# A transformer-style block chain with its residual stream kept token-major instead of feature-major

## The chip, the cores and the metric

One core of a Trainium2 chip. The metric is the device time of one execution in microseconds (us), the median of several runs. TensorE (PE) multiplies matrices, VectorE (DVE) and ScalarE (ACT) do the elementwise work, GpSimd (POOL) clears a few tiles, and SyncE (SP) issues nearly all DMAs.

## The reference, cut to what matters

256 tokens of 1024 features, all float32. Two layers of a first block, then one layer of a second block:

```python
h = x
for layer in range(2):
    xn = rms_norm(h, attn_norm_g[layer])
    ...                                   # SSM, spatial gating, differential attention
    h = h + mixed @ w_out[layer]          # 1024 x 1024
    xn = rms_norm(h, ffn_norm_g[layer])
    h = h + conv_gated_mlp(xn, w_up[layer], conv_w[layer], conv_b[layer], w_down[layer])   # w_down: 2816 x 1024
# second block: h2 = rms_norm(h, g_pre); three attention branches; merged; then
x = h + rms_norm(merged @ w_out_2, g_post)
```

The convolution runs along the tokens. The second block's attention over dilated windows is computed with the tokens in another order (t mod 4, t div 4 mod 4, t div 16).

## The kernel before

The program is traced through a scheduling layer that turns one list of operations into one instruction queue for each engine. Within a queue the order is fixed; between queues semaphores wait. Each operation has a priority, its place in the list; `later(tc, n)` moves it back by n places.

**Products.** Every large product is made exact by splitting both factors into a high and a low float32r part and adding three matmuls: high by high, high by low, low by high. The class `Stream` loads each weight by a 1 MB DMA on SP's queue (`wraw`, three buffers) and splits it in pieces of 128x1024 ahead of use: ACT writes `whi` (line 152), DVE writes `wlo` (line 153); there are five buffers of each, and four pieces are split ahead. Activations X are split in the same way into `xh` and `xl` (`split_scaled`, lines 664 and 665; `split_plain`, lines 668 and 669). All matmuls of a product go through `Bank.mm`, so they stand at line 94, and are told apart by their tiles: `acc` and `ps` are PSUM banks.

**Two layouts.** `mm_xs` makes token-major results: 128 tokens of X are stationary and 256 or 512 weight columns move. `mm_ws` makes feature-major ("d-major") results: a 128x128 piece of the weight is stationary and the 256 tokens of X move. The residual stream `h` is d-major, [128, 8, 256].

**w_out and w_down.** Both are written out inside `layer`, in the d-major manner: eight row blocks of w_out, or 22 of w_down (two for each j of `down`), times eight column blocks of 128, times three matmuls of 256 moving columns. Four banks `acc` collect the result. In layer 0, 16 identity matmuls first put x, turned to d-major, into the banks. In w_out one piece of the weight is used up after another; in w_down the two pieces of a j are held together while the banks are gone through one after the other.

**residual** (line 1198) follows each of these four products: a DVE addition for each bank (line 1206; none in layer 0's w_out, where ACT copies the bank at line 1216), the split into the next X (two for each bank), a Square on ACT (line 1213), a DVE addition of its halves (line 409), and in `Stats.add` two matmuls of one column against `ones` that sum the squares over the features. `Stats.finish` calls `norm_from`: the chain of small DVE operations of `rsqrt` (lines 373 to 383), two matmuls that spread the result over partitions (line 693), an ACT copy `rstdB` (line 696). The next products' results are scaled by `rstdB` or `rstd` when they are read out of PSUM; in the MLP that is the DVE operation of line 1342, which frees one of two `ps` banks.

**Around it.** After w_out comes `up(0)`, two products of 48 matmuls into the two `ps` banks. After layer 0's last `down`, `mem_keys` (96 matmuls) stands ahead of `residual`. After layer 1's last `down` comes the second block, whose `a_half` starts with products into `acc`; `x2_gen` (line 1440) transposes h back to token-major, 16 transposes and four copies, for the last addition. The token order of the second block is made by strided copies in layer 1: of h in `residual` (`permute`) and of the gated product in `up`. At the end, each tile q of 128 tokens is stored by two DMAs (line 1811) whose rows are picked out of the output in the other order.

Of the kernel before, what the change touches and what calls it, by code (L numbers as in the profile page):

```python
# [11 lines left out]
F32 = mybir.dt.float32  # L12
# [8 lines left out]
P = 128  # L21
S = 256
# [75 lines left out]
class Stream:  # L98
    """The weights in the order of their use: loaded, and split into two float32r parts, ahead of it."""
# [67 lines left out]
def tile_model(tc, t, out):  # L167
# [54 lines left out]
    # ------------------------------------------------------------------ weights in order of use  # L222
# [12 lines left out]
    # products of the mixers (lower case) and their generators' steps  # L235
# [58 lines left out]
    # ------------------------------------------------------------------ constants and small inputs  # L294
# [4 lines left out]
    ones = const.tile([P, 2], F32, name="ones")  # L299
    V.memset(ones, 1.0)  # L300
# [9 lines left out]
    def param_rows(*ps, eng=nc.sync):  # L310
        """Parameter rows -> columns of pvt."""
# [95 lines left out]
    # ------------------------------------------------------------------ first block: SSM parameters  # L407
# [12 lines left out]
    def ssm_params():  # L420
# [27 lines left out]
        # half angle -> full angle, then onto the unit circle  # L448
# [14 lines left out]
        # f = (a_bar - 1) / lambda  # L463
# [28 lines left out]
    def ssm_prep(l):  # L492
        """Segments of 4 tokens: A^i B-bar, C A^k, the 4-tap kernels Re(C A^i B-bar), the rotation table
        e^(-4 i theta m), m < 64, and the scan's multipliers."""
# [14 lines left out]
        def cmul(o, x, y, tv):  # L509
            """o = x * y for (re, im) pairs, tv scratch of o's shape."""  # L510
# [12 lines left out]
        # C^T, states on partitions, expanded with zeros and compact  # L523
# [15 lines left out]
        # powers of A, 0 to 4, and their products with f  # L539
# [23 lines left out]
        # C A^k, k from 1 to 4, the imaginary part negated  # L563
# [15 lines left out]
        # A^i B-bar; stacked as (channel, i) rows by states, and times C for the taps  # L579
# [40 lines left out]
        # rotation table  # L620
# [28 lines left out]
    # ------------------------------------------------------------------ token order of block 2  # L649
# [6 lines left out]
    # ------------------------------------------------------------------ normalisation helpers  # L656
# [14 lines left out]
    class Stats:  # L671
        """Sums of squares over d (rows of the d-major tiles) per token."""

        def __init__(self):
            self.b = psx()
            self.n = 0

        def add(self, sq):
            self.n += 1
# [5 lines left out]
        def finish(self):  # L685
# [1157 lines left out]
```

## Time and profile before

| | us |
|---|---|
| median of 3 runs (lowest, highest) | 1073.31 (1072.55, 1074.68) |
| span of the profiled execution, first to last instruction | 1071.4 |
| PE busy, and its weight loads (PEld) | 1028.5 and 956.9 |
| DVE busy, ACT busy | 779.0 and 624.1 |
| chain that ended last, share of PE | 85% |
| HBM read, over the span | 160.15 MB, 150 GB/s |

The profiled execution's time outside its span is not listed; its span is 1.9 us under the median of the runs. PE's busy time counts each matmul from its start to the end of its pipeline, so that neighbours overlap: what a matmul costs in a dense row is the distance between starts, read from a timeline or from a run of matmuls in the chain.

The stages stand in the span like this: layer 0's mixers to about 128 us, its w_out to 147.5, its MLP to 367.4, layer 1's mixers to 471, w_out to 487, MLP to 683.7, the second block to 1055.6, then the last norm and the stores.

### The profile page before, as it was taken

The numbers are of one execution on the slowest core, as the hardware profiler recorded it, in microseconds if no ns is written. First come the engines' busy times: TensorE is split into PE (matmuls) and PEld (weight loads), VectorE is DVE, ScalarE is ACT, GpSimd is POOL, SyncE is SP. The second block draws the span as 40 slices with busy tenths as digits, with TensorE's granted clock in tenths as the row PEclk, the third lists the DMA queues.
The fourth block names the chain that finished last, engine by engine and source line by source line (L and its number), as shares of the span: only waits on it lengthen the run. The fifth ranks groups of instructions, "written<-read, shape, count | busy, mean of one in ns | idle before, by whom it ended". The sixth has DMA issues, their size and how long they took to land.

```text
span 1071.4 us, 19616 instructions
## 1 busy us (share of the span) xinstructions
PE 1028.5 (96%) x7751; PEld 956.9 (89%) x7751; DVE 779.0 (73%) x1577; ACT 624.1 (58%) x1206; POOL 14.3 (1%) x34
## 2 busy tenths in 40 slices
PE   7799999999999999998999999999999999999994
PEld 5678898999999988888999999999787899899993
DVE  6978769877888769658878787876665666546663
ACT  5876567655665667657655555645675555444450
POOL 2000000000000000100000000000000000000000
PEclk9899999999999999999999999999999999999997
DMA  7542253555655445135556555468332546336531
GB/s 200 194 141 91 63 173 118 191 172 185 222 177 193 158 131 191 66 124 170 164 176 207 169 190 193 152 184 275 121 119 80 167 114 195 112 113 192 164 137 39
DMA packets 130484, 166.66 MB, mean 156 GB/s; under 512 B 12034, under 2 KB 103256, under 8 KB 130392
## 3 DMA queue, kind: packets, MB, share of 16 engines
q1 hardware_dynamic: 130360, 165.40, 47.9%
q8 instruction: 61, 1.00, 0.4%
q14 instruction: 31, 0.25, 0.1%
q10 hardware_dynamic: 32, 0.01, 0.0%
HBM read 160.15 MB, written 1.05 MB: 150 GB/s over the span
## 4 chain that ended last, share of the span: by engine, by line
PE 85%; DVE 7%; ACT 4%; issue 1%; DMA 1%; SPq 0%; POOL 0%; ACTq 0%; POOLq 0%; DVEq 0%
PE acc L94 50%; PE ps L94 26%; PE px L94 2%; DVE sgen L409 2%; DVE wlo L153 1%; PE pt L1506 1%; ACT sgen L600 1%; ACT whi L152 1%; ACT gen L1005 1%; PE px L905 1%; PE acc L1561 1%; DMA wraw<-in_w_in_dram 1%; PE acc L1652 1%; PE pt L1124 0%; DVE gen L1331 0%
## 5 line engine op out<-in xcount | busy, mean ns | idle before, releaser
L152 ACT ACTIVATE whi<-wraw 128x1024 fp32r<-128x1024 f32 x294 | 307.7, 1060 | 235.0 <-PE acc L94 112.5
L153 DVE TENSOR_TENSOR wlo<-wraw,whi 128x1024 fp32r<-128x1024 f32 x294 | 356.5, 1222 | 103.5 <-ACT whi L152 100.6
L94 PE MATMUL ps<-xh,whi 128*128 128x256 f32 x736 | 208.6, 285 | 3.7 <-DVE gen L1342 3.4
L94 PE MATMUL ps<-xl,whi 128*128 128x256 f32 x736 | 208.2, 283 | 0.8 <-DVE xl L665 0.8
L94 PE MATMUL ps<-xh,wlo 128*128 128x256 f32 x736 | 207.9, 283 | 0.0
L94 PE MATMUL acc<-xh,wlo 128*128 128x256 f32 x672 | 193.7, 289 | 4.0 <-DVE wlo L153 4.0
L94 PE MATMUL acc<-xh,whi 128*128 128x256 f32 x672 | 194.9, 291 | 1.2 <-ACT vm L1195 0.7
L94 PE MATMUL acc<-xl,whi 128*128 128x256 f32 x672 | 193.9, 289 | 0.5 <-DVE xl L669 0.5
L94 PEld LDWEIGHTS ps<-xh,whi 128*128 128x128 f32 x736 | 140.5, 191 | 4.4 <-DVE gen L1342 1.9
L94 PEld LDWEIGHTS ps<-xl,whi 128*128 128x128 f32 x736 | 140.8, 191 | 1.1 <-DVE xl L665 1.0
L94 PEld LDWEIGHTS ps<-xh,wlo 128*128 128x128 f32 x736 | 140.8, 191 | 0.0
L94 PEld LDWEIGHTS acc<-xh,wlo 128*128 128x128 f32 x672 | 129.6, 193 | 5.8 <-DVE wlo L153 4.7
L94 PEld LDWEIGHTS acc<-xh,whi 128*128 128x128 f32 x672 | 129.4, 193 | 4.7 <-issue 1.3
L94 PEld LDWEIGHTS acc<-xl,whi 128*128 128x128 f32 x672 | 129.5, 193 | 2.8 <-issue 1.5
L94 PE MATMUL acc<-whi,xh 128*128 128x512 f32 (+1 forms) x352 | 125.5, 358 | 3.0 <-ACT xh L664 2.6
L94 PE MATMUL acc<-wlo,xh 128*128 128x512 f32 (+1 forms) x352 | 125.8, 357 | 1.7 <-DVE wlo L153 1.6
L94 PE MATMUL acc<-whi,xl 128*128 128x512 f32 (+1 forms) x352 | 124.7, 355 | 0.0
L94 PE MATMUL acc<-al,whi 128*128 128x256 f32 x352 | 99.0, 281 | 0.5 <-DVE al L669 0.5
L94 PE MATMUL acc<-ah,whi 128*128 128x256 f32 x352 | 99.2, 282 | 0.0
L94 PE MATMUL acc<-ah,wlo 128*128 128x256 f32 x352 | 98.6, 281 | 0.0
L94 PEld LDWEIGHTS acc<-whi,xh 128*128 128x128 f32 x352 | 67.4, 191 | 11.7 <-ACT xh L664 3.5
L94 PEld LDWEIGHTS acc<-wlo,xh 128*128 128x128 f32 x352 | 67.4, 191 | 10.7 <-DVE wlo L153 2.6
(348 smaller groups left out, 1558.2 us busy)
## 6 DMA issues: line engine op xcount, KB each, us to landing
wraw<-in_w_in_dram SPq DMA_DIRECT2D x58, 1024.0 KB
wraw<-in_w_up_dram SPq DMA_DIRECT2D x44, 1024.0 KB
wraw<-in_w_down_dram SPq DMA_DIRECT2D x22, 1024.0 KB
wraw<-in_w_out_dram SPq DMA_DIRECT2D x12, 1024.0 KB
wraw<-in_w_mem_kv_dram SPq DMA_DIRECT2D x4, 1024.0 KB
gen<-gen SPq DMA_DIRECT2D x48, 64.0 KB
wraw<-in_w_br_b_dram SPq DMA_DIRECT2D x2, 1024.0 KB
wraw<-in_w_br_m_dram SPq DMA_DIRECT2D x2, 1024.0 KB
```

Of the source, the lines that this page charges most:

```text
L94: self.nc.tensor.matmul(out, lhsT=lhsT, rhs=rhs, start=not self.open, stop=stop)
L152: self.nc.scalar.activation(hv, part, AF.Copy)
L153: self.nc.vector.tensor_tensor(lv, part, hv.bitcast(F32), op=OP.subtract)
L409: (eng or V).tensor_tensor(o, a, b_, op=op)
L600: A.copy(pd[ps, hf], bpow[ri][ps, a * 4 : a * 4 + 4])
L905: T.matmul(bv[:, ri, q, :], lhsT=bt[:, ri, a, q * P : (q + 1) * P], rhs=u4[:, a * 4 + q, :], start=True, stop=True)
L1005: A.activation(sq[:, i * 64 : i * 64 + 64], src[:, i * 64 : i * 64 + 64], AF.Square, scale=rstd[:, q : q + 1], accum_out=ss[:, i : i + 1])
L1506: T.transpose(bk.t[:, i * P : (i + 1) * P], p[:, i * P : (i + 1) * P], ident)
L1561: T.matmul(oc, lhsT=pt[:, kt * P : (kt + 1) * P], rhs=vs[0][:, kt, cols], start=kt == 0, stop=False)
L1652: T.matmul(oc, lhsT=pt[:, (i * 2 + kt) * P : (i * 2 + kt + 1) * P], rhs=vb[:, kt, kv * 64 : kv * 64 + 64], start=kt == 0, stop=kt == 1)
```

## The change

Residual stream, w_out and w_down become token-major. `h` is now the tile `xraw` itself ([128, 2, 1024], where x was loaded), added to in place. A new helper `mm_tok` takes two pieces of weight together; for each half of the columns it makes 512-column matmuls with 128 tokens of X stationary, for both pieces and both token tiles, three each. `residual` adds a bank to h (DVE), squares and sums on ACT in one operation (`accum_out`), and makes the next X by transposes of h into PSUM, from which `split_scaled` reads. The second block's token order is made by the output pattern of the last residual's transposes (`tokens`), and undone by strided additions in the last merge. `Stats`, `ones`, the identity matmuls of x, `x2_gen` and the strided copies are gone. The final stores become one DMA of 128 rows for each tile.

```diff
-    class Stats:
-        def add(self, sq):
-            tt(sq[:, :S], sq[:, :S], sq[:, S:], OP.add)
-            for q in range(2):
-                self.b.mm(self.b.t[:, q : q + 1], sq[:, q * P : (q + 1) * P], ones[:, 0:1],
-                          stop=self.n == 4 and q == 1)
+    def tokens(ap, q, permute):
+        if not permute:
+            return ap[:, q * P : (q + 1) * P]
+        return flat_view(ap)[:, :, :, q * 8 : q * 8 + 8].rearrange("p a b c -> p c b a")
+
+    def norm_from(ss, permute=False):
...
+        if permute:
+            bk = pst()
+            for q in range(2):
+                T.transpose(bk.t[:, q * P : (q + 1) * P], rb[:, q * P : (q + 1) * P], ident)
+            rstd = small.tile([P, 2], F32, name=nm("rstd"), tag="rstd", bufs=2)
+            A.copy(rstd, bk.t[:, :S].rearrange("p (q c) -> p q c", q=2)[:, :, 0])
...
+    def residual(banks, h, gcol, X, permute=False):
+        parts = sm(4)
+        for n in range(2):
+            for q in range(2):
+                hv = h[:, q, n * 512 : n * 512 + 512]
+                tt(hv, banks[q][n].t, hv, OP.add)
+                A.activation(gen(), hv, AF.Square, accum_out=parts[:, q * 2 + n : q * 2 + n + 1])
+            for kp in range(2):
+                bk = psx() if kp else pst()
+                for kk in range(2):
+                    k = n * 4 + kp * 2 + kk
+                    for q in range(2):
+                        T.transpose(tokens(bk.t[:, kk * S : (kk + 1) * S], q, permute), h[:, q, k * P : (k + 1) * P], ident)
+                for kk in range(2):
+                    k = n * 4 + kp * 2 + kk
+                    split_scaled(X[0][:, k, :], X[1][:, k, :], bk.t[:, kk * S : (kk + 1) * S], pcol(gcol + k))
...
+    def mm_tok(banks, rows, last):
+        for n in range(2):
+            cols = slice(n * 512, n * 512 + 512)
+            for i, (xh, xl, hi, lo) in enumerate(rows):
+                for q in range(2):
+                    tok = slice(q * P, (q + 1) * P)
+                    b = banks[q][n]
+                    b.mm(b.t, xh[:, tok], hi[:, cols])
+                    b.mm(b.t, xh[:, tok], lo[:, cols])
+                    b.mm(b.t, xl[:, tok], hi[:, cols], stop=last and i == 1)
...
-        if l == 0:
-            for k in range(8):
-                for q in range(2):
-                    banks[k // 2].mm(banks[k // 2].t[...], xrv[:, q, k * P : (k + 1) * P], ident)
...
-            if last:
-                for n in range(2):
-                    sl = slice(n * S, (n + 1) * S)
-                    tt(flat_view(ac[:, sl]), perm_view(g_[:, sl]), perm_view(v_[:, sl]), OP.mult)
-            else:
-                tt(ac, g_, v_, OP.mult)
+            tt(ac, g_, v_, OP.mult)
...
-                    tt(mv, mv, y, OP.add)
+                    if bi_ == 2:
+                        mt = gen()
+                        for n in range(2):
+                            sl = slice(n * S, (n + 1) * S)
+                            tt(perm_view(mt[:, sl]), flat_view(mv[:, sl]), flat_view(y[:, sl]), OP.add)
+                        mv = mt
+                    else:
+                        tt(mv, mv, y, OP.add)
...
-    ov = out[0].rearrange("(c b a) d -> a b c d", b=4, a=4)
+    ov = out[0].rearrange("(q p) d -> q p d", p=P)
...
-        for al in range(2):
-            nc.sync.dma_start(ov[q * 2 + al], of[al * 64 : al * 64 + 64, :])
+        nc.sync.dma_start(ov[q], of)
```

The order of instructions at three places; line numbers after the change are those of the new program.

PE at the end of layer 0's w_out, before (`whi25` is the last piece of w_out, `ps` the first product of the MLP, `px` the sums of squares):

```order
L94 MATMUL acc_269_1572<-xh_191_1256,wlo25_1707 128x256
L94 MATMUL ps_288_1888<-xh_270_1822,whi26_1736 128x256
L94 MATMUL ps_288_1888<-xl_271_1823,whi26_1736 128x256
...
L94 MATMUL px_272_1824<-ones_92,gen_273_1829 128x1 x2
```

and after the change (`pt` and `px` now receive the transposes of h):

```order
L94 MATMUL acc_269_1570<-whi25_1639,xl_192_1255 128x512
L1205 MATMUL pt_275_1716<-ident_85,xraw_92 128x128 x4
L1205 MATMUL px_276_1725<-ident_85,xraw_92 128x128 x4
L94 MATMUL ps_293_1783<-xh_270_1707,whi26_1645 128x256
L94 MATMUL ps_299_1859<-xh_270_1707,whi28_1679 128x256
L94 MATMUL ps_293_1783<-xl_271_1708,whi26_1645 128x256
...
L1205 MATMUL pt_279_1740<-ident_85,xraw_92 128x128 x4
L1205 MATMUL px_280_1749<-ident_85,xraw_92 128x128 x4
```

Before, the product that follows starts at once; now eight transposes stand ahead of it, and eight more after its first eight matmuls.

DVE at the same place after the change (lines 407 add a bank to h, 663 write `xl`, 153 split a weight):

```order
L407 TENSOR_TENSOR xraw_92<-acc_267_1568,xraw_92 128x512
L153 TENSOR_TENSOR wlo29_1785<-wraw14_1643,whi29_1784 128x1024
L407 TENSOR_TENSOR xraw_92<-acc_269_1570,xraw_92 128x512
L663 SCALAR_TENSOR_TENSOR xl_271_1708<-pt_275_1716,pvt_95,xh_270_1707 128x256
L663 SCALAR_TENSOR_TENSOR xl_271_1708<-px_276_1725,pvt_95,xh_270_1707 128x256
L153 TENSOR_TENSOR wlo30_1823<-wraw15_1677,whi30_1822 128x1024
L663 SCALAR_TENSOR_TENSOR xl_271_1708<-pt_275_1716,pvt_95,xh_270_1707 128x256
```

Two splits of weights now stand among the additions and the splits of X; ACT has `whi30` just ahead of the first `xh` in the same way.

SP's last instructions, before:

```order
L1811 DMA out_0_dram<-o_1182_12141 4x16x1024 x2
L1811 DMA out_0_dram<-o_1185_12146 4x16x1024 x2
```

and after the change:

```order
L1787 DMA out_0_dram<-o_1200_11407 128x1024
L1787 DMA out_0_dram<-o_1203_11412 128x1024
```

The outermost extent of a store's pattern goes from 4 to 128.

## Rows read from the trace of the kernel before

**Rows 1.** The page: busy time, share of the span and instructions of each engine.
```profile
PE 1028.5 (96%) x7751; PEld 956.9 (89%) x7751; DVE 779.0 (73%) x1577; ACT 624.1 (58%) x1206; POOL 14.3 (1%) x34
```
**Rows 2.** The page: the chain that ended last, share of the span by engine.
```profile
PE 85%; DVE 7%; ACT 4%; issue 1%; DMA 1%; SPq 0%; POOL 0%; ACTq 0%; POOLq 0%; DVEq 0%
```
**Rows 3.** The chain in order of time (start us, us, what), layer 1's MLP.
```profile
517.03 5.68 PE acc L94 x48
522.72 11.50 PE ps L94 x96
```
**Rows 4.** PE's timeline (start us, us, what), the last product: first and last matmul.
```profile
1044.66 0.39 PE L94 MATMUL acc<-whi,xh 128*128 128x512 f32 x1
...
1055.31 0.39 PE L94 MATMUL acc<-whi,xl 128*128 128x512 f32 x1
```
**Rows 5.** The chain in order of time, layer 0's mixers and w_out.
```profile
92.86 1.34 PE acc L94 x12
...
94.42 2.44 PE acc L94 x21
...
128.12 19.60 PE acc L94 x164
```
**Rows 6.** Groups of PE's instructions by form: count, busy us, mean ns.
```profile
L94 PE MATMUL acc<-ident,xraw 128*128 128x128 f32 x32 | 4.4, 280 | 0.2 <-DVE ug L1264 0.2
L94 PE MATMUL px<-ones,gen 128*128 128x1 f32 x64 | 8.1, 237 | 0.0
```
**Rows 7.** Windows after each product, matmuls with `whi`: us, PE busy (count), clock.
```profile
147.50:166.00 18.50, 13.95 (x75) 1.00 0.53 171
367.40:380.60 13.20, 10.17 (x32) 1.00 0.49 159
486.80:506.50 19.70, 13.89 (x72) 1.00 0.47 157
683.70:700.00 16.30, 13.09 (x68) 1.00 0.43 136
```
**Rows 8.** PE's timeline after layer 1's w_out: the wait in brackets.
```profile
505.28 0.36 PE L94 MATMUL ps<-xh,whi 128*128 128x256 f32 x1 [1.74 <-DVE gen L1342]
```
**Rows 9.** PE's timeline, the transposes of h in the second block.
```profile
695.90 1.09 PE L1440 MATMUL pt<-ident,h 128*128 128x128 f32 x8
```
**Rows 10.** Timelines of DVE and ACT in layer 1's last residual: single operations.
```profile
684.64 0.87 DVE L665 SCALAR_TENSOR_TENSOR xl<-h,pvt,xh 128x256 fp32r<-128x256 f32 x2
685.77 0.68 DVE L1206 TENSOR_TENSOR h<-acc,h 128x512 f32<-128x512 f32 x1
686.37 2.35 DVE L153 TENSOR_TENSOR wlo<-wraw,whi 128x1024 fp32r<-128x1024 f32 x2
693.31 0.16 DVE L380 TENSOR_TENSOR sm<-sm 128x2 f32<-128x2 f32 x1
681.23 0.91 ACT L664 ACTIVATE xh<-h,pvt 128x256 fp32r<-128x256 f32 x2 [2.08 <-DVE h L1206]
685.21 2.00 ACT L152 ACTIVATE whi<-wraw 128x1024 fp32r<-128x1024 f32 x2
```
**Rows 11.** DMA from 1040 us to the end, in 40 slices of 0.8 us.
```profile
DMA  0000000000000000000022213222222222221000
GB/s 0 0 0 0 0 0 0 0 0 0 0 0 0 0 0 0 0 0 0 0 51 31 51 36 72 82 102 97 92 67 82 92 92 92 102 108 56 15 0 0
```
**Rows 12.** The same view of the first 15 us: loads of x and weights.
```profile
DMA  0000936979999999999999999997200000000762
GB/s 0 0 0 0 87 131 253 335 243 361 437 404 426 366 366 404 410 393 421 410 393 421 382 393 388 382 380 241 64 18 0 0 5 19 19 0 17 160 216 63
```
**Rows 13.** The tail: timelines of SP and DVE, SP's wait.
```profile
1054.85 6.55 SPq L1811 DMA_DIRECT2D out_dram<-o  x4
1058.97 1.28 DVE L1809 SCALAR_TENSOR_TENSOR o<-o,sm,x 128x1024 f32<-128x1024 f32 x1
SPq L1839 <- DMA out_dram<-o: 8.6, 1, 8.6
```

More of the change, by code (lines that the diff above doesn't have):

```diff
@@ L692, in norm_from @@
         for q in range(2):
-            T.matmul(bk.t[:, q * P : (q + 1) * P], lhsT=rstd[:, q : q + 1].to_broadcast([P, P]), rhs=ident,
+            T.matmul(tokens(bk.t[:, :S], q, permute), lhsT=rstd[:, q : q + 1].to_broadcast([P, P]), rhs=ident,
                      start=True, stop=True)
@@ L1195, in mem_values @@
             A.copy(vm[:, q, :], outs[q])
[L1198 to L1216 removed]
+    def residual(banks, h, gcol, X, permute=False):
[14 more added lines that the diff above has]
+                    split_scaled(X[0][:, k, :], X[1][:, k, :], bk.t[:, kk * S : (kk + 1) * S], pcol(gcol + k))
+        ss = sm(2)
+        pv_ = parts.rearrange("p (q n) -> p q n", q=2)
+        tt(ss, pv_[:, :, 0], pv_[:, :, 1], OP.add)
+        return norm_from(ss, permute)
+    def mm_tok(banks, rows, last):
[8 more added lines that the diff above has]
+                    b.mm(b.t, xl[:, tok], hi[:, cols], stop=last and i == 1)
     def layer(l, h, X, norm):
@@ L1287, in layer @@
         low[0] = 0
-        banks = [acc() for _ in range(4)]
-        if l == 0:
-            for k in range(8):
-                for q in range(2):
-                    banks[k // 2].mm(banks[k // 2].t[:, (k % 2) * S + q * P : (k % 2) * S + (q + 1) * P],
-                                     xrv[:, q, k * P : (k + 1) * P], ident)
-            h = hpool.tile([P, 8, S], F32, name="h0", tag="h")
-        for ki in range(8):
-            k = OUT_ORDER[l][ki // 2] + ki % 2
-            hi, lo = st.take()
-            mx = mix
-            for bi in range(4):
-                for n in range(2):
-                    cols = slice((bi * 2 + n) * P, (bi * 2 + n + 1) * P)
-                    o = banks[bi].t[:, n * S : (n + 1) * S]
-                    banks[bi].mm(o, hi[:, 0, cols], mx[0][:, k, :])
-                    banks[bi].mm(o, hi[:, 0, cols], mx[1][:, k, :])
-                    banks[bi].mm(o, lo[:, 0, cols], mx[0][:, k, :], stop=ki == 7 and n == 1)
-            step()
+        banks = [[acc(), acc()] for _ in range(2)]
+        for k in OUT_ORDER[l]:
+            rows = []
+            for kk in range(2):
+                hi, lo = st.take()
+                rows.append((mix[0][:, k + kk, :], mix[1][:, k + kk, :], hi[:, 0, :], lo[:, 0, :]))
+            mm_tok(banks, rows, k == OUT_ORDER[l][-1])
+            step(2)
         last = l == LAYERS - 1
         X = new_x()
-        stats = Stats()
-        residual(banks, h, FG + l * 8, X, stats, last, l == 0)
-        last = l == LAYERS - 1
-        rstd, rb = stats.finish()
+        rstd, rb = residual(banks, h, FG + l * 8, X)
         rb2 = rb.unsqueeze(1).to_broadcast([P, 2, S])
         st.split_later = (SPLIT_F0, SPLIT_F1)[l]
-        banks = [acc() for _ in range(4)]
+        banks = [[acc(), acc()] for _ in range(2)]
         if not last:
@@ L1360, in down @@
             subs = [st.take(), st.take()]
-            for bi in range(4):
-                for n in range(2):
-                    cols = slice((bi * 2 + n) * P, (bi * 2 + n + 1) * P)
-                    o = banks[bi].t[:, n * S : (n + 1) * S]
-                    for kk in range(2):
-                        hi, lo = subs[kk]
-                        sl = slice(kk * S, (kk + 1) * S)
-                        banks[bi].mm(o, hi[:, 0, cols], ah[:, sl])
-                        banks[bi].mm(o, hi[:, 0, cols], al[:, sl])
-                        banks[bi].mm(o, lo[:, 0, cols], ah[:, sl], stop=j == 10 and n == 1 and kk == 1)
+            rows = []
+            for kk in range(2):
+                hi, lo = subs[kk]
+                sl = slice(kk * S, (kk + 1) * S)
+                rows.append((ah[:, sl], al[:, sl], hi[:, 0, :], lo[:, 0, :]))
+            mm_tok(banks, rows, j == 10)
             step()
@@ L1382, in layer @@
         Xo = new_x()
-        stats = Stats()
-        residual(banks, h, GP if last else AG + 8, Xo, stats)
-        return h, Xo, stats.finish()
+        return Xo, residual(banks, h, GP if last else AG + 8, Xo, last)
     def chain(*gs):
@@ L1393, in tile_model @@
     for l in range(LAYERS):
-        h, X, norm = layer(l, None if l == 0 else h, X, norm)
+        X, norm = layer(l, xrv, X, norm)
     b1.close()
@@ L1430, in tile_model @@
     V.tensor_scalar(rstdh, rstd, 0.5, None, op0=OP.mult)
-    x2 = const2.tile([P, 2, D], F32, name="x2")
-    def x2_gen():
-        for q in range(2):
-            for half in range(2):
-                bk = pst()
-                for k in range(4):
-                    T.transpose(bk.t[:, k * P : (k + 1) * P], h[:, half * 4 + k, q * P : (q + 1) * P], ident)
-                A.copy(x2[:, q, half * 512 : half * 512 + 512], bk.t)
-                yield
     def qt_tile():
@@ L1704, in tile_model @@
     st.split_later = SPLIT_B2
-    fill.append(x2_gen())
     qts, vs = a_half(0, 1)
@@ L1738, in tile_model @@
     fill.append(ga_)
-    merged = hpool.tile([P, 8, S], F32, name="merged", tag="h")
+    merged = const2.tile([P, 8, S], F32, name="merged")
     XMG = None
```

30 lines of the change are left out of this document (1 added, 29 removed).

## Prediction

> **What bounds the kernel now.** I read the page first: PE is busy for 96% of the span and its weight loads for 89% [rows 1]; the chain that ended last belongs to PE for 85% [rows 2]. So what counts is the distance between PE's matmuls, and the few places where PE waits. The chain in order of time gives the first: in the MLP PE goes from `ps` to `acc` and back without a pause, 48 matmuls of w_down in 5.68 us, 118.3 ns each, and 96 of w_up in 11.50 us, 119.8 ns each [rows 3]. The dense row of 512-column matmuls is the last product: 48 starts from 1044.66 to 1055.31, 47 distances of 226.6 ns [rows 4]. Two matmuls of 256 columns thus take 236.6 to 239.6 ns, one of 512 takes 226.6: some 11 ns per matmul do not depend on the columns. The waits stand where one product ends and the next needs its norm (four residuals), and at the end, where the stores last 8.6 us for SP after all computing is done [rows 13].
>
> **The change part by part**, against the profiled span of 1071.4 us (the median of the runs is 1.9 us longer, and I carry that along).
>
> *w_down.* For each of 22 j (11 in each layer) 48 matmuls of 256 become 24 of 512: 24 x 0.2266 = 5.44 us for 5.68 [rows 3, 4]. 22 x 0.24 = **-5.3 us**, all on PE's path, since nothing waits in these stretches.
>
> By the rule of the Trainium skill (TensorE: Matmul & The Clock Gate, section "Wait — 56ns, not 53.3ns?"), the start-to-start distance is columns / 2.4 GHz plus about 2.5 ns, which makes 215.8 and 109.2 ns and a gain of only 2.6 ns for each merged pair; by it w_down would give 1.4 us. The rows show about 11 ns of fixed cost, where each matmul has its own weight load, and the sum goes by them.
>
> *w_out.* The same step, 192 matmuls of 256 to 96 in each layer. In layer 0 the chain holds 164 records in 19.60 us, 119.5 ns [rows 5], eight of them identity records; the other 156 become 78 x 0.2266 = 17.7 us instead of 18.6. I take as many in layer 1: **-1.9 us**. The matmuls placed earlier fill waits of the mixers; if they paid too it would be -2.4.
>
> *x into layer 0's banks.* 32 records (two for each float32 matmul) at about 0.112 us apart go: 3.6 us of PE. 16 of them lie in the two runs of the chain at 93 to 97 us and eight in the one at 128 us, while the other eight stand off the chain [rows 5, 6]: 24 x 0.112 = **-2.7 us**, at least 0.9 (the eight that begin w_out) and at most 3.6.
>
> *The four residuals.* First their price now: in the windows after each product, two thirds of the weight matmuls carry `whi`, so 75, 72 and 68 stand for 112, 108 and 102 matmuls of 119.7 ns, and 32 for 48 of 226.6 [rows 7]. Window less matmuls: 5.1 (layer 0 w_out), 2.3 (layer 0 w_down, covered by `mem_keys`), 6.8 (layer 1 w_out) and 4.1 us (layer 1 w_down), 18.3 in all. In them lie the sums of squares (64 records, [rows 6]), the wait for `rstdB` (DVE, line 1342), which frees a `ps` bank (1.74 us in layer 1, [rows 8]), and in the last one the 16 transposes of h, eight in about 1.1 us [rows 9].
>
> Then the price after, with T the end of the product. PE has eight transposes first: the half n = 0 was finished 12 matmuls (2.7 us) before T, so they run at once, to T + 1.1. ACT has a split `whi30` ahead of the first `xh`, and its buffer comes free only at T, because a pair of pieces is now held to its end: 1.0 + 0.45 us [rows 10], so the first matmul starts at about T + 1.6. DVE adds the last bank (0.68) behind a split of 1.2, so the first `xl` is there at about T + 2.0; then a second `xl` (0.44), another split of a weight (1.2) and two more `xl`, until T + 4.5. Only then are the banks `pt` and `px` free for the other eight transposes, and PE, which had eight matmuls (1.0 us) to do meanwhile, goes on at T + 5.1. Loss 4.1. The chain of small DVE operations (ten of 0.16 to 0.2, four `xl` between them) ends at T + 8.2; PE reaches its broadcast after 22 more matmuls, at T + 7.7: 0.6 of wait and 0.4 for the broadcast. That is 5.1; with the four transposes of the next layer's preparation, which stand in the old figure too, 5.5 in layer 0; 4.9 in the last residual, where 12 matmuls stand between, and a second pair of transposes follows the broadcast. Behind `mem_keys` the additions are long done, but `whi100` waits for that product's buffer in the same way, and all the X splits stand behind it: first matmul at T + 2.1, 1.0 of transposes later, 0.3 of broadcast: 3.4. Sum 18.9 for 18.3: **+0.6 us**. Bounds: if only the 16 transposes showed, 4 x 2.2 = 8.8, a gain of 9.5; if one more split of a weight (2.2 us on ACT and DVE together) came ahead in each, a loss of 9.4. I stay near the middle, where the orders put it.
>
> *Elsewhere.* The strided additions of the last merge (eight of 256 columns for four of 512) add some 0.3 us ahead of the last product's last two blocks, which PE reaches only after six of eight, 36 matmuls or 8.2 us: nothing. DVE loses the strided pairs of layer 1 and the halves' additions, and gains four additions in layer 0; it is at 73% and pays nothing.
>
> *The stores.* The last DVE operation ends at 1060.25 and the span at 1071.4, 11.1 us later [rows 13]. The stores of 0.5 MB for each tile flow at 92 GB/s or less, at two tenths of the 16 DMA engines, and the first tile's is not done when the second's is issued [rows 11]. The load of x, [128, 1024] by [128, 1024], just what a store is after the change, runs in the stretch at 360 to 430 GB/s at nine tenths [rows 12]. At 390 GB/s 0.5 MB takes 1.3 us instead of 5.7, and the first tile's is gone before the second starts. From issue to first data 1.3 us (1054.85 to the slice at 1056), 1.3 us of data, 1.2 us from the last data to the end: 3.8 for 11.1. If the slow start seen in the first four slices (42 GB/s, here times four) held all through, the data would take 3.1 us and the gain be 5.5. I take **-6.5 us**, between 5.5 and 7.3.
>
> The Trainium skill (DMA: Bandwidth & Descriptors, section "Why a DMA increments its semaphore by 16 and not by 1") says why: the number of engines is the largest k up to 16 that divides both patterns' slowest extents, here 4 before and 16 after. The two tenths in the trace agree with four of 16.
>
> Sum: -5.3 - 1.9 - 2.7 + 0.6 - 6.5 = -15.8, so 1055.6 for the span and **1057.5 us** for the median.
>
> **The rivals.** (a) *The stores keep their rate*, because writing to HBM, not the pattern, is slow: -9.3, 1064.0. For it: no row shows a store of another shape. Against: the share of two tenths, and first data at a sixth of the loads' rate. 0.08. (b) *The residuals wait longer*, one split of a weight more in front of X: +9.4 on top, about 1066 to 1067. For it: five buffers and pairs held to the end. 0.10. (c) *They wait less*, 1.5 us each: 1051.5. For it: sums of squares on ACT need no PE and start a half earlier. 0.10. (d) *A matmul with its own weight load costs its columns alone*, so that merging gives 2.6 ns instead of 10: w_down and w_out give 1.9 for 7.2, 1062.8. Against it the two dense rows. This is where the skill's rule on the distance would lead. 0.03. (e) *Slower*: the splits of weights fall behind because a pair holds two of five buffers to its end. If in each of the 30 pairs the next pair's second piece came a whole split (2.2 us) too late, it would cost 66 us; it decides from the point where ACT or DVE have over 5.4 us of work in a pair's time, for the splits take 2.0 and 2.4 of it. Only in w_out is the pairing new (w_down held two pieces before); eight pairs and four residuals there would be 26 us, 1084. 0.03. (f) *The merge does nothing and the residuals eat the rest*: 1073. 0.01.
>
> **How the numbers follow.** The forecast has 0.65 and spans 1054 to 1061 by itself. The range takes in (a), (c) and (d), and the lower part of (b): **1051.5 to 1065.0**. 0.2%, 2.1 us, is about what a measurement can tell. Faster by more than that: all but (e) and (f), 0.96; within it 0.01; slower 0.03.
>
> **What would show it.** Right: w_down's 24 matmuls in 5.4 us in the chain; 7 to 8 tenths or more of DMA share and over 250 GB/s in the last stretch, with the span ending 4 to 6 us after the last DVE operation; after each w_out, PE waiting for `xh` and `xl` for about 3 to 4 us and hardly for `rstdB`. Wrong: a distance well over 227 ns in w_down; PE waiting for `whi` or `wlo` within the pairs; windows after the residuals that lose over 7 us each; a store that still takes 5 us.

## The result, and the profile after

The changed kernel takes 1062.18 us (median of 4 runs, 1061.41 to 1064.08), the kernel before 1073.05 in the same comparison; the ratio is 0.9895, with a 95% interval of 0.9881 to 0.9909. That is 10.9 us faster, inside the range, 4.7 us above the forecast. The profiled execution has a span of 1059.2 us for 1071.4. It is the shortest of the four: the other spans are 1059.5 to 1061.9, and each run's time is 2.2 us over its span. So 3.6 us of the 4.7 are missing in the span itself, and 1.1 in how the median stands to the execution that was profiled.

The page of the changed kernel, busy time and then the chain's shares (as [rows 1, 2] of before):

```profile
PE 1019.6 (96%) x6985; PEld 913.6 (86%) x6985; DVE 773.0 (73%) x1561; ACT 618.1 (58%) x1207; POOL 14.3 (1%) x34
PE 80%; DVE 4%; ACT 3%; issue 1%; SPq 0%; DMA 0%; POOL 0%; ACTq 0%; POOLq 0%
```

PE has 766 matmuls fewer and is still what bounds the kernel. Where the 12.2 us of span come from is read by following the same instruction through both timelines; the gain so far is the difference of the two starts, and the last two columns give what each step gained, and what the prediction had for it.

| moment | before | after | gained so far | in this step | predicted |
|---|---|---|---|---|---|
| first of the SSM's 126 small matmuls, layer 0 | 119.13 | 119.15 | 0.0 | 0.0 | 1.8 |
| ACT copies their bank | 125.04 | 126.39 | -1.35 | -1.3 | 0 |
| end of w_out, layer 0 | 147.56 | 147.02 | 0.54 | 1.9 | 1.8 |
| first matmul of w_down | 175.86 | 175.54 | 0.32 | -0.2 | -0.4 |
| end of w_down | 355.73 | 354.46 | 1.27 | 0.9 | 2.6 |
| `px<-sgen,bt` in layer 1's mixers | 400.13 | 399.34 | 0.79 | -0.5 | -1.1 |
| end of w_out, layer 1 | 486.82 | 484.40 | 2.42 | 1.6 | 1.0 |
| first matmul of w_down | 516.87 | 512.54 | 4.33 | 1.9 | 1.7 |
| end of w_down | 683.69 | 678.23 | 5.46 | 1.1 | 2.6 |
| `gen<-gen,csa` in the second block | 707.60 | 702.69 | 4.91 | -0.5 | -0.8 |
| last DVE operation | 1058.97 | 1054.03 | 4.94 | 0.0 | 0 |
| end of the span | 1071.4 | 1059.2 | 12.2 | 7.2 | 6.5 |

Below, the lead of one run over another means the same thing: how much earlier the same instruction starts.

Three steps fall short: the identity matmuls, a new loss of 1.3 us at the SSM's bank, and w_down, twice. The chain of the changed kernel in layer 1's MLP shows the last (start us, us, what):

```profile
512.70 5.60 PE acc L94 x24
518.30 11.51 PE ps L94 x96
```

w_up takes what it took [rows 3], but w_down's 24 matmuls take 5.60 us, 233.3 ns each, and not the 226.6 of the last product [rows 4].

The loss at the SSM's bank is seen on ACT: timelines of the changed kernel, and of the kernel before (waits in brackets).

```profile
118.10 0.20 ACT L1121 ACTIVATION_READ_ACCUMULATOR gen<-pt 128x1 f32 x1
125.09 1.28 ACT L942 ACT_TABLE_LOAD   x1 [6.79 <-issue]
126.39 0.60 ACT L942 ACTIVATE sgen<-acc 128x512 f32<-128x512 f32 x1
```

```profile
117.63 1.28 ACT L948 ACT_TABLE_LOAD   x1 [1.25 <-DVE sm L375]
125.04 0.60 ACT L948 ACTIVATE sgen<-acc 128x512 f32<-128x512 f32 x1 [6.13 <-PE acc L94]
```

Before, the table for the Gelu was loaded while PE filled the bank, and only the Gelu waited for PE. Now the load itself begins when PE is done.

The first step of the table, where the identity matmuls should have paid, is seen on PE: before the change, and after it.

```profile
119.13 5.87 PE L94 MATMUL acc<-sgen,ct 128*32 128x64 f32 x126
119.15 5.87 PE L94 MATMUL acc<-sgen,ct 128*32 128x64 f32 x126 [1.20 <-DVE sgen L407]
```

Before, PE came to these matmuls without a pause; the last DVE operation whose result they need had run from 118.26 to 118.94 and so ended 0.2 us ahead of them. After the change PE is there earlier and waits 1.20 us for that operation.

On the table load, the Trainium skill (ScalarE: Activation LUTs, section "What ACT_TABLE_LOAD costs") gives about 1283 ns for the load and 1380 for a drain; the first agrees, and of the second nothing is seen here: the Gelu starts 0.02 us after the load.

The residual after layer 0's w_out, on PE (the product ends at 147.02):

```profile
147.02 0.60 PE L1205 MATMUL pt<-ident,xraw 128*128 128x128 f32 x4
147.46 0.60 PE L1205 MATMUL px<-ident,xraw 128*128 128x128 f32 x4
148.75 0.50 PE L94 MATMUL ps<-xh,whi 128*128 128x256 f32 x2 [0.69 <-ACT xh L662]
149.41 0.38 PE L94 MATMUL ps<-xl,whi 128*128 128x256 f32 x1 [0.16 <-DVE xl L663]
150.70 0.50 PE L94 MATMUL ps<-xh,whi 128*128 128x256 f32 x2 [0.55 <-ACT xh L662]
151.42 0.63 PE L1205 MATMUL pt<-ident,xraw 128*128 128x128 f32 x4 [0.22 <-DVE xl L663]
152.24 0.36 PE L94 MATMUL ps<-xl,whi 128*128 128x256 f32 x1
155.17 0.68 PE L681 MATMUL pt<-ident,rstd 128*128 128x128 f32 x4
```

This is the working of the prediction nearly to the tenth: first matmul 1.7 us after the end (1.6 forecast), PE goes on behind the second transposes after 5.2 (5.1), the broadcast comes after 8.2 (8.2). The sign that was named for it did not show as written: the waits for `xh` and `xl` in brackets are 1.6 us in all, not 3 to 4.

The tail (DMA from 1040 us to the end in 40 slices of 0.48 us, then the last DVE operation):

```profile
DMA  0000000000000000000000599100000003994000
GB/s 0 0 0 0 0 0 0 0 0 0 0 0 0 0 0 0 0 0 0 0 0 0 222 410 410 51 0 0 0 0 0 0 0 137 401 401 171 0 0 0
1054.03 1.28 DVE L1786 SCALAR_TENSOR_TENSOR o<-o,sm,xraw 128x1024 f32<-128x1024 f32 x1
```

Each tile's 0.5 MB flow at 400 GB/s with nine tenths of the engines, and the span ends 3.9 us after the last DVE operation (3.8 forecast, 11.1 before [rows 11, 13]).

### The profile page after: what moved, and what is told of

Read it like the earlier page. It is cut to its first block, busy times and chain, and to the rows that moved or that the text cites. A ratio compares the mean times of both kernels' runs of the same rounds, so it can differ in the third digit from the quotient of the medians.

```text
span 1059.2 us, 18058 instructions
## 1 busy us (share of the span) xinstructions
PE 1019.6 (96%) x6985; PEld 913.6 (86%) x6985; DVE 773.0 (73%) x1561; ACT 618.1 (58%) x1207; POOL 14.3 (1%) x34
## 4 chain that ended last, share of the span: by engine, by line
PE 80%; DVE 4%; ACT 3%; issue 1%; SPq 0%; DMA 0%; POOL 0%; ACTq 0%; POOLq 0%
PE acc L94 48%; PE ps L94 26%; PE pt L1476 1%; DVE wlo L153 1%; PE px L94 1%; PE acc L1531 1%; DVE sgen L407 1%; PE acc L1622 1%; ACT whi L152 1%; ACT sgen L598 0%; ACT gen L999 0%; PE acc L1533 0%; PE px L899 0%; PE px L948 0%; PE acc L1663 0%
## 5 line engine op out<-in xcount | busy, mean ns | idle before, releaser
L94 PE MATMUL acc<-xh,wlo 128*128 128x256 f32 x544 | 157.9, 290 | 4.3 <-DVE wlo L153 4.3
L94 PE MATMUL acc<-xh,whi 128*128 128x256 f32 x544 | 158.3, 292 | 0.8 <-ACT xh L662 0.7
L94 PE MATMUL acc<-xl,whi 128*128 128x256 f32 x544 | 157.1, 289 | 0.1
L94 PE MATMUL acc<-whi,xh 128*128 128x512 f32 (+1 forms) x416 | 150.2, 364 | 6.0 <-ACT xh L662 3.4
L94 PE MATMUL acc<-wlo,xh 128*128 128x512 f32 (+1 forms) x416 | 151.3, 364 | 1.9 <-DVE wlo L153 1.8
L94 PE MATMUL acc<-whi,xl 128*128 128x512 f32 (+1 forms) x416 | 150.0, 362 | 0.0
L94 PEld LDWEIGHTS acc<-xh,whi 128*128 128x128 f32 x544 | 105.0, 193 | 3.2 <-issue 1.3
L94 PEld LDWEIGHTS acc<-wlo,xh 128*128 128x128 f32 x416 | 79.5, 191 | 13.7 <-DVE wlo L153 3.4
L94 PEld LDWEIGHTS acc<-whi,xl 128*128 128x128 f32 x416 | 79.1, 190 | 10.0 <-DVE xl L663 0.3
L94 PE MATMUL acc<-whi,ah 128*128 128x512 f32 x176 | 69.9, 397 | 0.3 <-ACT ah L666 0.3
L94 PE MATMUL acc<-wlo,ah 128*128 128x512 f32 x176 | 69.5, 395 | 0.0
```

The costliest lines, as they stand in the source:

```text
L94: self.nc.tensor.matmul(out, lhsT=lhsT, rhs=rhs, start=not self.open, stop=stop)
```

## The experiments

Two causes were open: what slows w_down's matmuls, and why the table load now waits. Besides, the terms on the stores, the residuals and the identity matmuls were each taken apart. All times are compared with the kernel before on the same chip; spans are of the profiled executions.

### w_down: addresses or neighbours

Between the two kernels `ones`, a tile of 128x2, is gone from the first pool, and with it 32 bytes in each partition; these are addresses of the two programs, not of a trace. All tiles that are allocated behind it moved down by 32 bytes. Before, X, `whi` and `wlo` started 32 bytes off a multiple of 64, and `ah`, `al` on one. After, X and the weights are on multiples of 64 and `ah`, `al` are 32 off.

**e1_work64**

```diff
     const1 = b1.enter_context(tc.tile_pool(name="const1", bufs=1))
+    const1.tile([P, 8], F32, name="pad_c1")
```

> Edit: 32 bytes of padding in the pool const1, so that the tiles of the pool work1 (ah and al among them) start on multiples of 64 bytes again; X and the split weights stay where they are, on multiples of 64. Theory A (addresses): w_down's 24 matmuls of 512 columns fall from 5.60 to 5.44 us (233 to 226.6 ns each), 22 x 0.16 = 3.5 us off the span of 1059.2. Rival B (what DVE and ACT do beside w_down slows its matmuls): 5.60 us stay, the span moves by less than 0.5 us.

Measured: 1059.79 us (ratio 0.9884, 0.9869 to 0.9898), span 1057.9. The chain at the same place:

```profile
512.70 5.47 PE acc L94 x24
518.16 11.51 PE ps L94 x96
```

w_down falls to 5.47 us at nearly every j (one in layer 0 takes 5.74, for 5.76). The lead over the changed kernel grows by 1.15 us in layer 0's w_down and by 1.33 in layer 1's, 2.5 in all for the 3.5 expected. The span shows 1.3 of it: the lead was 1.15 us at 468 us and nothing at 496, since here the granted clock fell behind layer 1's w_out (last section). The intervals of the two ratios overlap; it is the chain that decides. Neighbours on DVE and ACT did the same work as before, so theory B falls.

**e2_w32_work32**

```diff
     wpool = es.enter_context(tc.tile_pool(name="wsplit", bufs=5))
+    wpool.tile([P, 8], F32, name="pad_w", tag="padw", bufs=1)
...
+    const1.tile([P, 8], F32, name="pad_c1")
```

> Edit: padding that puts the split weights (whi, wlo) 32 bytes off a multiple of 64; ah and al stay 32 off, X stays on a multiple of 64. Theory A1 (what counts is whether both operands of a matmul have the same offset modulo 64): w_down falls to 5.44 us (both 32 off), w_out rises from 226.6 to 233 ns (96 x 6.7 ns = 0.6 us in each layer), and the products of 256 columns with X moving fall from 119.8 to the 118.3 ns that w_down had before the change, 2112 of them in w_up alone: 3.1 us; span near 1052 to 1054. Theory A2 (only the stationary operand's own offset counts): w_down stays at 5.60 us, w_out and w_up as they are, span 1059. Rival B (work beside it): nothing moves.

Measured: 1055.77 us (ratio 0.9846, 0.9832 to 0.9861), span 1054.3. Its chain, in layer 0's w_out and in the MLP:

```profile
129.25 17.51 PE acc L94 x75
...
512.09 5.46 PE acc L94 x24
517.54 11.36 PE ps L94 x96
```

and the changed kernel's w_out, at the same place:

```profile
129.47 17.05 PE acc L94 x75
```

All three moved as A1 said: w_down to 5.46, w_out from 227.3 to 233.5 ns a matmul, w_up's 96 from 11.51 to 11.36 us. A2 and B fall. The span is just over the 1052 to 1054 us expected; here too the granted clock fell behind layer 1's w_out, and 1.2 us of the lead went there. So it is the difference of the operands' starts: with equal offsets modulo 64 a matmul of 512 columns takes 226.6 ns and one of 256 takes 119.8; 32 bytes apart they take 233.3 and 118.3. Across the two kernels, e2 and e11, each of the four cases occurs twice: the equal ones with both tiles on a multiple of 64 and with both off it, the unequal ones with the one tile off it and with the other. So it is not the offset of one tile that counts.

**e11_before_w64**

The same padding of `wsplit` in the kernel before (X 32 off, weights on a multiple of 64).

> Edit: the kernel before with 32 bytes of padding ahead of whi and wlo, which puts these on multiples of 64 bytes and ah and al 32 off; X stays 32 off. Theory (unequal offsets of the two operands make a matmul of 256 columns 118.3 instead of 119.8 ns, and one of 512 233 instead of 226.6): w_up's 96 matmuls in 11.36 us instead of 11.50, 22 x 0.14 = 3.1 us; w_out 0.6 us; w_down stays at 5.68; with the second block's products, as e2 had them (about 1.6 us), some 5 us in all: span 1066. Rival (the gain of e2 belongs to the changed kernel): span 1071.

Measured: 1068.95 us (ratio 0.9960, 0.9945 to 0.9974), span 1067.0. Its chain:

```profile
515.94 5.68 PE acc L94 x48
521.62 11.36 PE ps L94 x96
```

w_up falls to 11.36 us in the other kernel too, and w_down stays at 5.68, as expected. The span is 4.4 us shorter for some 5 expected; here too the granted clock fell behind layer 1's w_out, where 1.5 us of the lead were lost. The figures also say what the merge is worth: 118.3 x 2 for 226.6 where each form has its better addresses, 10 ns a pair; as the change was made, w_down went from its better ones (118.3) to its worse (233.3), 3.3 ns a pair.

### The table load

**e3_gelu_early**

```diff
+        early = small.tile([P, 1], F32, name=nm("early"), tag="early", bufs=1)
+        A.activation(early, ident[:, 0:1], AF.Gelu_apprx_tanh)
         A.activation(yg, yb.t, AF.Gelu_apprx_tanh)
```

> Edit: one ACT operation of one column with the same function as the Gelu of line 942, right ahead of it, which waits for nothing, so that the table load comes before the wait for the bank of the SSM. Theory: in layer 0 the load (1.28 us) runs at about 118 us while PE fills the bank, the copy of the bank starts at 125.0 instead of 126.4 us, and everything behind is 1.3 to 1.4 us earlier: span 1057.9. Rival: the 1.3 us are taken up again by the wait for the weight splits at w_out or at the residual: span within 0.3 us of 1059.2.

Measured: 1066.12 us (ratio 0.9940, 0.9925 to 0.9954), span 1062.2, slower than the changed kernel. Its ACT timeline, the table loads:

```profile
10.04 1.28 ACT L943 ACT_TABLE_LOAD   x1
...
36.87 1.28 ACT L838 ACT_TABLE_LOAD   x1
...
128.24 1.28 ACT L944 ACT_TABLE_LOAD   x1
```

The experiment missed its aim. An operation that waits for nothing was put at 10 us by the scheduling layer, which cost two loads there and left the third where it was. It says nothing on the theory.

**e5_gelu_l0**

```diff
+        if l == 0:
+            early = small.tile([P, 1], F32, name=nm("early"), tag="early", bufs=1)
+            A.activation(early, st_[1][:, 7, 0:1], AF.Gelu_apprx_tanh)
         A.activation(yg, yb.t, AF.Gelu_apprx_tanh)
```

> Edit: in layer 0 alone, an ACT operation of one column with the Gelu's function, which reads one column of the last SSM state (ready at about 118.4 us) and stands ahead of the Gelu of line 942; its tile moves ah and al to multiples of 64 bytes, so the kernel to compare with is e1_work64 (span 1057.9, of which about 1.2 us are a stretch at the lower granted clock). Theory: the table load (1.28 us) runs at about 118.5 to 119.8 us beside PE's 126 small matmuls, the copy of the bank starts at 125.0 instead of 126.2 us, and all that follows is 1.2 to 1.4 us earlier: span about 1056.6, or 1055.4 without a stretch at the lower clock. Rival: the gain is taken back by w_out's weights or by the residual: under 0.4 us against e1.

Measured: 1058.49 us (ratio 0.9859, 0.9843 to 0.9876), span 1055.1. ACT's timeline:

```profile
117.86 1.28 ACT L944 ACT_TABLE_LOAD   x1
119.15 0.20 ACT L944 ACTIVATE early<-sgen 128x1 f32<-128x1 f32 x1
124.66 0.60 ACT L945 ACTIVATE sgen<-acc 128x512 f32<-128x512 f32 x1 [5.30 <-PE acc L94]
```

The load is hidden again. The lead over the changed kernel is 0.46 us at 121.7 and 1.73 at 151.8: 1.27 us gained at this place, and kept: the lead is still 1.74 us where w_down begins. The median is 1.3 us under e1's (measured in another comparison).

**e10_before_no_identity**

```diff
-            for k in range(8):
-                for q in range(2):
-                    banks[k // 2].mm(banks[k // 2].t[...], xrv[:, q, k * P : (k + 1) * P], ident)
```

> Edit: the kernel before, without the 16 identity matmuls that bring x into layer 0's banks (x is so left out of the residual stream). Theory 1 (their price in the prediction): 2.7 us less, span 1068.7. Theory 2 (the stretch at 93 to 119 us is bound by the chain on DVE that ends in the SSM's states; only the eight at the head of w_out, 0.9 us, count; and the table load before the Gelu of line 948 now stands behind the wait for PE, 1.3 us): the 126 small matmuls of the SSM begin at 119.1 as before, the copy of their bank at 126.3 instead of 125.0, span 1071.4 - 0.9 + 1.3 = 1071.8.

Measured: 1075.08 us (ratio 1.0017, 1.0008 to 1.0026), span 1073.1: taking 32 records away does not make the kernel before faster. Its PE and ACT timelines:

```profile
119.52 5.87 PE L94 MATMUL acc<-sgen,ct 128*32 128x64 f32 x126 [0.53 <-DVE sgen L409]
```

```profile
125.46 1.28 ACT L948 ACT_TABLE_LOAD   x1 [6.79 <-issue]
126.76 0.60 ACT L948 ACTIVATE sgen<-acc 128x512 f32<-128x512 f32 x1
```

PE waits for DVE ahead of the small matmuls, and these begin no earlier (119.52 for 119.13; this execution was 0.27 late at 90 us already). That time is not clean: the granted clock was 0.51 and 0.63 in the two stretches of 2 us from 112 us, and 1.00 in the kernel before and in the changed kernel. But in the changed kernel, at the full clock, the matmuls begin no earlier either (119.15), and behind a longer wait. Then the load moves behind PE, as in the changed kernel. So this removal alone does both. Over the head of w_out, where the last eight records are gone, the lag behind the kernel before shrinks from 1.72 to 0.83 us: these 0.9 us are real. The span is 1.3 us over theory 2's sum; the clock may be part of that, since its ten runs have mean clocks of 0.986 to 0.990 and those of the kernel before 0.990 to 0.993.

In the program's ACT queue the reason for the late load can be read. Before, the order is: the wait for DVE, the table load, the Gelu with the wait for PE. With the identity matmuls gone the Gelu gets a third wait, on ACT's own counter (its output seems to take a buffer that ACT used last), and the order is: the waits for DVE and PE, the table load, the Gelu with the wait for ACT. The changed kernel's queue has this same order. Theory 1 (2.7 us) falls.

### The stores

**e4_old_stores**

```diff
-    ov = out[0].rearrange("(q p) d -> q p d", p=P)
+    ov = out[0].rearrange("(c b a) d -> a b c d", b=4, a=4)
...
-        nc.sync.dma_start(ov[q], of)
+        for al in range(2):
+            nc.sync.dma_start(ov[q * 2 + al], of[al * 64 : al * 64 + 64, :])
```

> Edit: only the final stores are as before the change, two DMAs for each tile with 4x16x1024 as pattern; all computing stays, and the rows of the output come out in another order. Theory (the pattern sets how many DMA engines work): 7.2 us from the last DVE operation to the end of the span come back: 11.1 us instead of 3.9, span 1066.4, a DMA share of two tenths in the tail. Rival (the tail is shorter because the rows come out of other tiles or at another time): less than 2 us come back.

Measured: 1069.20 us (ratio 0.9967, 0.9954 to 0.9979), span 1068.1. The last 19.1 us of its DMA, in 40 slices:

```profile
DMA  0000000002221322212222222222222221111000
GB/s 0 0 0 0 0 0 0 0 0 51 51 34 43 51 43 60 69 77 86 94 103 112 103 94 103 86 112 103 86 103 112 112 103 69 51 51 51 0 0 0
```

Two tenths are back, and the span ends 10.6 us after the last DVE operation instead of 3.9: 6.7 of the 7.2 us hang on how the stores are cut, their pattern and their number together.

**e8_stores_64**

```diff
+        for al in range(2):
+            nc.sync.dma_start(ov[q][al * 64 : al * 64 + 64, :], of[al * 64 : al * 64 + 64, :])
```

> Edit: each tile is stored by two DMAs of 64 whole rows (64x1024) instead of one of 128. Theory (the slow stores of before come from the outermost extent of 4, not from the number of DMAs): from the last DVE operation to the end 3.9 us, within 0.4. Rival (each further DMA costs, whatever its pattern): 5 us or more.

Measured: 1063.18 us (ratio 0.9902, 0.9882 to 0.9922), span 1061.3. The last 19.3 us of its DMA:

```profile
DMA  0000000000000000000029899200000299892000
GB/s 0 0 0 0 0 0 0 0 0 0 0 0 0 0 0 0 0 0 0 0 59 212 161 212 357 85 0 0 0 0 0 59 212 170 238 348 77 0 0 0
```

Neither theory alone: the engines are at eight to nine tenths as with 128 rows, but move 160 to 240 GB/s for most of the time, and the tail is 5.1 us. Why they move less at the same share was not tried. The pattern's outermost extent brings 5.5 us of the gain (10.6 to 5.1), the single DMA another 1.2.

### The residuals

**e6_early_transposes**

```diff
+    def residual(*a):
+        with later(tc, -300):
+            return residual_(*a)
```

> Edit: all operations of the residual get a priority 300 places earlier, so that the eight transposes of the first half of h stand among the last twelve matmuls of the product (after two and four of them) and the first X splits stand ahead of the weight splits that were ahead of them. Theory (the waits for the first xh and xl, 0.89 + 0.32 + 0.71 + 0.38 us in layer 0, come from the splits of weights that stand ahead): PE goes from the product to the next with the 16 transposes and the broadcast as its only loss; 1.2 to 2 us less in each of three residuals, span about 1054 to 1056. Rival: the transposes now wait inside the product for DVE's additions (0.7 us each), so that the waits move and less than 1 us is gained in all.

Measured: 1057.03 us (ratio 0.9845, 0.9830 to 0.9859), span 1055.0. PE at the end of layer 0's w_out:

```profile
147.57 0.39 PE L94 MATMUL acc<-whi,xl 128*128 128x512 f32 x1
147.79 0.28 PE L94 MATMUL ps<-xh,whi 128*128 128x256 f32 x1
...
149.66 0.30 PE L1209 MATMUL pt<-ident,xraw 128*128 128x128 f32 x1 [0.64 <-DVE xl L663]
```

The next product starts without a pause, and the one wait left here is that for `pt`, which holds the first X pieces. Against the changed kernel 1.2, 0.9, 1.6 and 0.3 us come back in the four residuals, 4.2 less span in all: the theory, at its lower end and once under it.

**e7_early_acc**

```diff
-                bk = psx() if kp else pst()
+                bk = acc()
```

(with e6, and the four banks taken in the order in which the additions free them)

> Edit: e6, and the transposes go into the four acc banks that the additions have just freed, not into pt and px. Theory (the second eight transposes wait for the X splits to free pt and px, 0.4 us in each residual): another 0.3 to 0.6 us less in each residual than e6, 1 to 2 us in all. Rival: these eight are late because of the second half's additions, not of the banks: same as e6 within 0.5 us.

Measured: 1056.64 us (ratio 0.9843, 0.9828 to 0.9858), span 1055.9. In layer 0's w_out 3.1 us come back instead of 1.2, in the next two 1.1 and 1.6; but the last residual loses 2.4. PE there:

```profile
675.51 0.33 PE L1209 MATMUL acc<-ident,xraw 128*128 128x128 f32 x1 [1.85 <-DVE xraw L407]
...
678.33 0.41 PE L94 MATMUL acc<-xl,whi 128*128 128x256 f32 x1
```

PE waits 1.85 us for an addition, and the matmuls after it stand some 0.21 us apart (eleven distances from 678.33 to 680.68) instead of 0.12: the granted clock was at its lower level there, 0.50 from 678 to 680 us. How much of the 2.4 us is the clock's was not separated, and the profiled execution is the slowest of e7's four (spans 1053.8 to 1055.9, mean clock 0.991 here and 0.995 in the two fastest). So the theory holds in layer 0's w_out, the rival in the next two residuals, and on the last the runs leave it open.

### All three together

**e9_combined**: the edits of e5 and e6, the padding of `wsplit` (with e5's tile, it leaves `ah` and `al` 32 off), and

```diff
-                bk = psx() if kp else pst()
+                bk = acc() if not permute else psx() if kp else pst()
```

> Edit: the changed kernel with three things together: whi, wlo, ah and al 32 bytes off a multiple of 64 and X on one (as e2), the small Gelu in layer 0 (as e5), and the early residual (as e6) with the transposes in the freed acc banks after w_out and layer 0's w_down, in pt and px in layer 1's last residual. Theory (the three are independent, since they act on different stretches): 6.3 us from e2 (its stretch at the lower clock left out), 1.3 from e5, 6.1 from e7 and e6 (3.1, 1.1 and 1.6 us in three residuals, 0.3 in the last): 13.7 less than 1059.2, a span of 1045.5, median 1047 to 1048. Rival (PE's time saved in the residuals is lost again, because the splits of weights, pushed back by X, come too late): span over 1049, with PE waiting for whi or wlo in the first products after each residual.

Measured: 1047.17 us (ratio 0.9757, 0.9743 to 0.9772), span 1044.9. Its chain in the MLP:

```profile
503.17 5.44 PE acc L94 x24
508.62 11.36 PE ps L94 x96
```

The parts add up (14.3 for 13.7), as they should if they are independent, and this version is 1.4% faster than the changed kernel and 2.4% than the one before.

## Why the prediction was right, and where it was off

*Right in direction and range, and in its largest term.* The stores gave 7.2 us for 6.5. The rate of the load of x, the same pattern in the other direction, was a sound price for a store never seen. Rival (a) falls. That the gain splits into 5.5 us for the pattern and 1.2 for the single DMA (e4 and e8) was not in the working. The rule of the Trainium skill that the prediction cites (DMA: Bandwidth & Descriptors, section "Why a DMA increments its semaphore by 16 and not by 1") agrees as far as shares show it: eight to nine tenths for an extent of 128 or 64, two for 4.

*The residuals*: -0.2, -0.5, +1.9 and -0.5 make a gain of 0.7 for a forecast loss of 0.6; each is within 0.6 of its own figure, and all four came out better than forecast. Writing the order of ACT, DVE and PE against the end of the product was worth its length. The bounds, 9 us to either side, were far too wide for it, and rivals (b) and (c) fall.

*w_down is the step that failed*: "48 matmuls of 256 become 24 of 512: 24 x 0.2266 = 5.44 us for 5.68". The 0.2266 came from the last product, whose operands start at equal offsets modulo 64; w_down's do not. It measured 5.60, 0.08 a j for 0.24, and 3.2 us of the 5.3 did not come (2.1 came, by the table above). e1 and e2 show the cause, and e1 gets 2.5 of the 3.2 back. At equal offsets 5.47 us are left, 8.8 ns gained for each pair; so rival (d), whose 2.6 ns would give 5.62, was nearly matched by number and for another reason. The rule of the Trainium skill on the distance (TensorE: Matmul & The Clock Gate, section "Wait — 56ns, not 53.3ns?") doesn't hold for these matmuls, each of which loads its own weight: 226.6 and 119.8 ns stand against its 215.8 and 109.2.

*The x identity matmuls* measured 0.9 of 2.7, the bound named as the least. The step that failed is that two runs of matmuls in the chain at 93 to 97 us were taken as PE's price, though the chain behind them passes to DVE and ACT several times before 119 us; what is saved ahead of such a passage waits there. The 1.20 us that PE waits at 119.15 in the changed kernel show it, and e10, where this removal is the only edit, shows the same wait (0.53 us, beside the lower clock). Before the change the DVE operation was done just 0.2 us ahead of PE, at 118.94, and after it no earlier, at 119.10; so an earlier PE could win nothing there.

*Not foreseen*: 1.3 us for the table load. No row of before shows a wait that the load could inherit, but both programs were there to be read, and the waits of the Gelu in them were not compared.

*w_out* gave 1.6 us in layer 1, more than the 0.95 that the share of the chain gave, which counted only the 78 merged matmuls of layer 0's chain. All 96, with those placed in the mixers, make 1.2 at some 12 ns each (two at 119.7 for one at 227); the text had that as a bound (2.4 for both layers). The other 0.4 was not traced. Rival (e) falls: PE waited for no weight within the pairs of w_out and w_down. The page's groups show it (count | busy, mean ns | idle before); the first is w_down's, the second holds w_out's beside other products, and its waits for `wlo` stand at 28.70 and 35.08 us, in layer 0's mixers.

```profile
L94 PE MATMUL acc<-wlo,ah 128*128 128x512 f32 x176 | 69.5, 395 | 0.0
L94 PE MATMUL acc<-wlo,xh 128*128 128x512 f32 (+1 forms) x416 | 151.3, 364 | 1.9 <-DVE wlo L153 1.8
```

The sum, by its terms: w_down 3.2 short, identities 1.8 short, table load 1.3 lost; w_out, residuals and stores 2.7 over: 3.6 short. That is the 3.6 us of span, so the total came out nearer than its terms: 6.3 us of misses against 2.7 the other way.

## What to carry to other kernels

Take the pace of a matmul only from rows of the same form and the same tiles, and after any edit that adds or drops a small tile look at where the operands start: 32 bytes here were worth 2.5 us in one product (e1) and 5 in the kernel (e2). After a removal compare the waits of the instructions that stayed, above all of an ACT operation that switches tables: a wait that moved ahead of the load cost the load here, 1.3 us. Transposes between two products paid among the last matmuls of the first, as soon as half of its columns were done, with the splits of the next operand ahead of those of the weights: 4.2 us over four residuals (e6).

## What the runs showed of the hardware that was not expected

*Operand offsets.* The pace of a float32r matmul with its own weight load depended on whether the moving and the stationary tile start at the same offset modulo 64 bytes, in opposite senses for the two widths (512 columns: 226.6 equal, 233.3 unequal; 256 columns: 119.8 and 118.3). Offsets other than 0 and 32 were not tried, and why the two widths differ in sense is not known.

*The clock behind a lean residual.* In e1, PE was busy for 1.1 and 1.2 us of the two stretches of 2 us behind layer 1's w_out, and the granted clock fell to its lower level (1.2 GHz, 0.50) in the next one. Windows of e1 (us, PE, PEld, DVE, ACT, POOL busy, clock, DMA share, GB/s):

```profile
484.00:486.00 2.00, 1.09 (x7) 0.64 (x6) 2.00 (x5) 2.00 (x6) 0.00 (x0) 1.00 0.12 23
486.00:488.00 2.00, 1.23 (x8) 0.85 (x7) 2.00 (x5) 1.22 (x4) 0.00 (x0) 0.84 0.85 301
488.00:490.00 2.00, 2.00 (x11) 2.00 (x10) 1.16 (x6) 0.80 (x2) 0.00 (x0) 0.50 0.53 209
```

and of the changed kernel:

```profile
484.00:486.00 2.00, 1.44 (x11) 1.07 (x9) 2.00 (x3) 1.88 (x4) 0.00 (x0) 1.00 0.22 73
486.00:488.00 2.00, 1.25 (x6) 0.83 (x6) 2.00 (x4) 2.00 (x8) 0.00 (x0) 1.00 0.48 76
488.00:490.00 2.00, 1.66 (x13) 1.48 (x14) 1.82 (x8) 0.88 (x4) 0.00 (x0) 1.00 1.02 422
```

The same stretch had the lower clock in the profiles of e2, e4, e8 and e11, and it cost about 1.2 us in e1. That such stretches also make the spread of the changed kernel's own runs is likely: spans of 1059.2, 1059.5, 1060.4 and 1061.9 us go with mean clocks of 0.994, 0.992, 0.991 and 0.989. It was not shown, since only the first was profiled. In e9, where PE's leanest stretch of 2 us there holds 1.4 us of work, the clock stayed full; but it stayed full at 1.25 in the changed kernel too, so these runs do not tell when the clock falls.
